# A pad of 256 instead of 192 bytes in front of the second and third stage's tiles

## The chip, the core and the metric

The kernel runs on one core of a Trainium2 chip. The metric is the device time of one execution in microseconds (us); lower is better. The core has five engines with instruction queues of their own: TensorE (PE, matrix multiply; its weight loads are listed as PEld), VectorE (DVE), ScalarE (ACT), GpSimd (POOL) and SyncE (SP), which issues the DMAs here. Matmuls read both operands from SBUF, 128 partitions of on-chip memory, and write PSUM. A tile in SBUF has the same byte address in every partition, and "its address" below means that.

## What is computed

One layer of an encoder on 2048 tokens of width 1024 in float32: three token mixers on one normalised input, merged by gates, projected into the residual stream, and an MLP.

```
h = rmsnorm(x, g_mix);  z = h @ w_in
h_m   = bidirectional chunkwise mLSTM (4 heads)
h_na  = 2-D neighbourhood attention (8 heads, 32 x 64 grid)
h_mem = cross-attention into 256 memory tokens (4 heads)
gates = sigmoid(gate_pre)
y = gates[0] * (h_m @ w_proj_mlstm) + gates[1] * (h_na @ w_proj_na) + gates[2] * (h_mem @ w_proj_mem)
x = x + y @ w_out
u = rmsnorm(x, g_ffn) @ w_up                    # 1024 -> 4096
return x + square(relu(u)) @ w_down             # 4096 -> 1024
```

## The kernel before

Every large product is taken in the type fp32r with each operand split in two, high part and rest, and three matmuls (high x high, high x rest, rest x high). `mm3` issues them on lines 232, 233 and 234. In `matmul(out, lhs, rhs)` the left operand is the stationary one (128x128, loaded as weights), the right one is moving (128x512). The profile's names give the moving operand first: `mm<-X,ws` streams from X against weights of a ws tile. Where both operands are in the same tile one name stands, `mm<-X`. Lines 232 and 233 share a stationary operand, 234 has the rest part.

The work runs in three stages, each with a pool of tiles of its own in the same part of SBUF (`p1`, `p2`, `p3` in `phases`):

- Stage 1 (`phase_1`): normalisation, the projections of `w_in` block by block (512 tokens each), the attention branches. `tok_group` has moving ws and stationary hT, `ch_group` moving hT and stationary ws.
- Stage 2 (`phase_2`): the mLSTM (`ml_stream`, many small matmuls on the stage's own tiles, lines 773 to 905), and between them the gates of two blocks by `ch_group`.
- Stage 3 (`phase_3`): gates left over (`late_gates`), and then for each of two pairs of blocks: `merge` (8 chunks of 128 channels; branches against projection weights, moving X, stationary ws), `out_proj` (32 groups of 24 matmuls over both pairs; moving ws, stationary hT or X; each followed by four transposes on line 1341 that make operands of the MLP), `mlp_up` (16 rounds) and `mlp_down`.

The MLP's two products are done as 2x2 block products with 7 instead of 8 multiplications. `mlp_up` takes its left operands (weights and their sums) from ws tiles and its right operands from X; one product is 4 k-steps of three matmuls. `mlp_down` takes both from X, where its operands are loaded and split on lines 1463 and 1464. In these loops the order of TensorE's instructions is the order of the program (`manual_schedule`).

What the places in SBUF are:

- The pool `ws` comes first: a pad of 128 bytes at byte 1152, then five buffers of 8448 bytes from 1280 on.
- The pool `h`: hT, 32768 bytes at 43520. The outputs of mlp_up and the sums of mlp_down (`acc`) take its place in turn, and so does the merge's result for one block of a pair.
- The pool `w` (raw weights, three buffers of 4224 bytes) at 76288, the pool `c` (identity, constants, small tiles) at 88960.
- At 96768 begin `p1`, `p2` and `p3` in turn. `p2` and `p3` begin with a pad of `PAD` bytes (`self.pad(self.p_a, PAD)` in `phases`), which is a tile of its own, set to zero once on DVE (line 251). In `p3` the next tile is X: seven places of 2 (high, rest) x 4 x 512 numbers, 114688 bytes. With 192 bytes of pad X begins at 96960. Behind it come small tiles and the eight buffers `ev`.

Slices of these tiles that matmuls read begin whole multiples of 512 bytes into the tile in X, ws and hT alike.

The right operands of the MLP in the code:

```
        def product(p, l, r, first):                                  # mlp_up
            lhs, rhs = w[l], self.X[r]
            for k in range(4):
                self.mm3(p, (lhs[0][:, k], lhs[1][:, k]), (rhs[:, 0, k], rhs[:, 1, k]), ...)
...
                        self.mm3(p, (at[:, 0, d, ts], at[:, 1, d, ts]), (at[:, 0, 2 + d], at[:, 1, 2 + d]), ...)   # mlp_down
```

Of the kernel before, what the change touches and what calls it, by code (L numbers as in the profile page):

```python
# [23 lines left out]
TB = 512  # L24
LOW, LATER, LATER_A, SOON = 100, 60, 60, 40
TICKS_2, START_2 = 4, 20
PAD = 192
EV = {1: 2, 2: 2, 3: 8}
XT = 2
PREP_V = 2  # L30
# [50 lines left out]
class Body:  # L81
# [176 lines left out]
    def phases(self):  # L258
# [7 lines left out]
        with tc.tile_pool(name="p2", bufs=1) as self.p_a:  # L266
            self.pad(self.p_a, PAD)
            self.ev_bufs = EV[2]
            self.psum(self.phase_2, mm=2, pn=4, mx=2)
        with tc.tile_pool(name="p3", bufs=1) as self.p_a:  # L270
            self.pad(self.p_a, PAD)
            self.ev_bufs = EV[3]
# [1305 lines left out]
```

## Time and profile before

| | |
|---|---|
| median of 3 runs | 2993.33 us (2991.52 to 2995.25) |
| the profiled execution | 2998.03 us |
| its span, first to last instruction | 2996.3 us |
| mean granted TensorE clock | 0.994 |
| weights, intermediates and results moved by DMA | 632.97 MB, mean 211 GB/s |

The page lists for each engine its busy time, its share of the span and its instructions; then the chain of work that ended last, followed back from the end; then groups of instructions by line: operation, tiles (output and inputs), shape, count, busy time, mean duration, and idle time of the engine before them with what ended it. A matmul's bar is longer than the distance to the next matmul, since they are pipelined: the timeline (start, length, engine, line, operation) shows starts, and the view by windows gives busy time and counts within chosen stretches, the granted clock, and the mean busy share of the 16 DMA engines.

### The profile page before, as it was taken

How to read it: one execution, taken by the hardware profiler on the slowest of the kernel's cores; microseconds unless marked ns; L12 is line 12 of the kernel's file. 1: busy time of each engine (PE TensorE's matmuls, PEld its weight loads, DVE VectorE, ACT ScalarE, POOL GpSimd, SP SyncE). 2: the span in 40 equal slices, each digit the busy share in tenths (PEclk: the TensorE clock that was granted, in tenths of full speed). 3: DMA queues.
4: the chain of work that ended last, by engine and by line, in shares of the span. 5: the costliest groups of instructions: out<-in, count | busy, mean ns of one | idle time of the engine just before them, and what ended most of it. 6: DMA issues, size and time to landing. Idle time of an engine off the chain costs nothing.

```text
span 2996.3 us, 41916 instructions
## 1 busy us (share of the span) xinstructions
PE 2929.4 (98%) x15028; PEld 2375.1 (79%) x15028; DVE 2066.5 (69%) x3523; ACT 1195.8 (40%) x2198; POOL 268.8 (9%) x423
## 2 busy tenths in 40 slices
PE   8999999999989899999999999999999999999999
PEld 6888888778777677778888888888778888888887
DVE  6676864476654766765688878666675987885665
ACT  6465654355543333342243333533312433334331
POOL 4121200021001323420000000000000000000000
PEclk9999999999999999999999999999999999999999
DMA  8786877876998667788444445766863444466554
GB/s 276 222 275 200 242 231 246 275 215 203 289 283 267 199 202 236 247 275 306 141 132 161 144 149 178 256 195 218 280 209 119 148 151 146 142 223 226 191 185 165
DMA packets 341712, 632.97 MB, mean 211 GB/s; under 512 B 29344, under 2 KB 151008, under 8 KB 341504
## 3 DMA queue, kind: packets, MB, share of 16 engines
q1 hardware_dynamic: 341504, 630.30, 65.5%
q8 instruction: 118, 1.93, 0.3%
q14 instruction: 90, 0.74, 0.1%
HBM read 453.63 MB, written 176.55 MB: 210 GB/s over the span
## 4 chain that ended last, share of the span: by engine, by line
PE 55%; DVE 2%; DMA 2%; issue 1%; ACT 0%; POOL 0%; SPq 0%; DVEq 0%; ACTq 0%; POOLq 0%
PE mm L232 18%; PE mm L233 18%; PE mm L234 18%; PE mm L1341 0%; DMA wr<-in_w_units_dram 0%; DMA hf<-s_hf 0%; DVE h L901 0%; DMA og<-s_o 0%; DVE ev L1497 0%; DVE acc L1490 0%; ACT hf L897 0%; POOL rs L325 0%; DMA X<-s_a 0%; DVE ws L177 0%; DVE h L889 0%
## 5 line engine op out<-in xcount | busy, mean ns | idle before, releaser
L232 PE MATMUL mm<-X,ws 128*128 128x512 f32 x1152 | 455.7, 396 | 0.0
L234 PE MATMUL mm<-X,ws 128*128 128x512 f32 x1152 | 455.4, 395 | 0.0
L233 PE MATMUL mm<-X,ws 128*128 128x512 f32 x1152 | 455.4, 395 | 0.0
L232 PE MATMUL mm<-hT,ws 128*128 128x512 f32 x896 | 375.0, 419 | 8.2 <-DMA hT<-s_hT 4.4
L177 DVE TENSOR_TENSOR ws<-wr,ws 128x1024 fp32r<-128x1024 f32 (+1 forms) x212 | 264.5, 1254 | 136.2 <-ACT ws L176 132.6
L234 PE MATMUL mm<-hT,ws 128*128 128x512 f32 x896 | 353.2, 394 | 0.0
L233 PE MATMUL mm<-hT,ws 128*128 128x512 f32 x896 | 353.2, 394 | 0.0
L233 PE MATMUL mm<-X 128*128 128x512 f32 x896 | 349.6, 390 | 3.4 <-DVE X L1464 3.4
L234 PE MATMUL mm<-X 128*128 128x512 f32 x896 | 349.3, 390 | 0.5 <-DVE X L1464 0.5
L232 PE MATMUL mm<-X 128*128 128x512 f32 x896 | 349.3, 390 | 0.0
L1463 ACT ACTIVATE X<-X 128x1024 fp32r<-128x1024 f32 x176 | 186.6, 1062 | 324.7 <-DMA X<-s_t 115.7
L1464 DVE TENSOR_TENSOR X<-X 128x1024 fp32r<-128x1024 f32 x176 | 214.6, 1224 | 136.7 <-ACT X L1463 135.8
L176 ACT ACTIVATE ws<-wr 128x1024 fp32r<-128x1024 f32 (+1 forms) x212 | 223.4, 1058 | 163.8 <-PE mm L234 88.9
L232 PE MATMUL mm<-ws,hT 128*128 128x512 f32 (+2 forms) x704 | 259.8, 369 | 2.7 <-ACT zif L524 1.8
L234 PEld LDWEIGHTS mm<-X,ws 128*128 128x128 f32 x1152 | 216.4, 188 | 52.3
L232 PEld LDWEIGHTS mm<-X,ws 128*128 128x128 f32 x1152 | 216.4, 188 | 52.2
L233 PEld LDWEIGHTS mm<-X,ws 128*128 128x128 f32 x1152 | 216.5, 188 | 52.1
L234 PE MATMUL mm<-ws,hT 128*128 128x512 f32 (+2 forms) x704 | 249.6, 355 | 2.0 <-DVE hT L434 2.0
L233 PE MATMUL mm<-ws,hT 128*128 128x512 f32 (+2 forms) x704 | 248.9, 354 | 0.0
L202 ACT ACTIVATE ws<-wr 128x512 fp32r<-128x512 f32 x224 | 135.1, 629 | 229.8 <-PE mm L234 148.8
L232 PEld LDWEIGHTS mm<-hT,ws 128*128 128x128 f32 x896 | 170.1, 190 | 49.7 <-issue 10.7
L234 PEld LDWEIGHTS mm<-hT,ws 128*128 128x128 f32 x896 | 169.6, 189 | 38.9
(266 smaller groups left out, 4865.8 us busy)
## 6 DMA issues: line engine op xcount, KB each, us to landing
wr<-in_w_units_dram SPq DMA_DIRECT2D x308, 512.0 KB
s_s<-u SPq DMA_DIRECT2D x32, 1024.0 KB
X<-s_s SPq DMA_DIRECT2D x64, 512.0 KB
X<-s_t SPq DMA_DIRECT2D x64, 512.0 KB
s_g<-ev SPq DMA_DIRECT2D x96, 256.0 KB
ev<-s_g SPq DMA_DIRECT2D x96, 256.0 KB
s_a<-u SPq DMA_DIRECT2D x96, 256.0 KB
X<-s_a SPq DMA_DIRECT2D x48, 512.0 KB
```

The source lines that it names most:

```text
L176: nc.scalar.activation(w[:, 0], raw, AF.Copy)
L177: nc.vector.tensor_tensor(w[:, 1], raw, w[:, 0].bitcast(F32), ALU.subtract)
L202: nc.scalar.activation(hi, src, AF.Copy)
L232: mm(out, lhs[0], rhs[0], start=first, stop=False)
L233: mm(out, lhs[0], rhs[1], start=False, stop=False)
L234: mm(out, lhs[1], rhs[0], start=False, stop=last)
L1463: nc.scalar.activation(hi, src, AF.Copy)
L1464: nc.vector.tensor_tensor(lo, src, hi.bitcast(F32), ALU.subtract)
```

## The change

The constant `PAD` is 256 instead of 192. It is the size in bytes of the pads at the start of `p2` and `p3`. All tiles of the second and the third stage lie 64 bytes higher; X begins at 97024. Tiles of the pools `ws`, `h`, `w` and `c` and of stage 1 stay where they are. No instruction is added or removed; the two pads' memsets write 64 instead of 48 columns.

```
@@ -24,7 +24,7 @@
 TB = 512
 LOW, LATER, LATER_A, SOON = 100, 60, 60, 40
 TICKS_2, START_2 = 4, 20
-PAD = 192
+PAD = 256
 EV = {1: 2, 2: 2, 3: 8}
 XT = 2
 PREP_V = 2
```

More of the change, by code (lines that the diff above doesn't have):

```diff
@@ L26 @@
 TICKS_2, START_2 = 4, 20
-PAD = 192
+PAD = 256
 EV = {1: 2, 2: 2, 3: 8}
```

## The prediction

> **What bounds the kernel now.** I read the page from the top: engines, then the chain that ended last.
>
> ```profile
> span 2996.3 us, 41916 instructions
> PE 2929.4 (98%) x15028; PEld 2375.1 (79%) x15028; DVE 2066.5 (69%) x3523; ACT 1195.8 (40%) x2198; POOL 268.8 (9%) x423
> PE 55%; DVE 2%; DMA 2%; issue 1%; ACT 0%; POOL 0%; SPq 0%; DVEq 0%; ACTq 0%; POOLq 0%
> L232 PE MATMUL mm<-X,ws 128*128 128x512 f32 x1152 | 455.7, 396 | 0.0
> L232 PE MATMUL mm<-X 128*128 128x512 f32 x896 | 349.3, 390 | 0.0
> ```
>
> The third line is the chain: it was followed back over some 60% of the span, and 55 of these 60 points are TensorE. So a matmul that gets shorter shortens the kernel, as long as nothing else is late. The groups name the moving operand first, then the stationary one. `mm<-X,ws` (X streams, weights come from a ws tile) is merge and mlp_up: 1152 on each of the lines 232, 233 and 234, 3456 in all. `mm<-X` (both operands in X) is mlp_down, 2688 in all.
>
> Busy time says little here, since a matmul's bar is 0.39 us and the next one starts long before it ends. What counts is the step from start to start. The timeline of TensorE gives it wherever an unbroken stretch begins and ends:
>
> ```profile
> 1377.34 0.39 PE L232 MATMUL mm<-X,ws 128*128 128x512 f32 x1
> 1466.94 0.39 PE L232 MATMUL mm<-ws,hT 128*128 128x512 f32 x1
> 1567.55 0.47 PE L232 MATMUL mm<-X,ws 128*128 128x512 f32 x1
> 1875.62 0.39 PE L232 MATMUL mm<-X 128*128 128x512 f32 x1
> 2187.05 0.40 PE L232 MATMUL mm<-X,ws 128*128 128x512 f32 x1
> 2276.64 0.39 PE L232 MATMUL mm<-ws,yT 128*128 128x512 f32 x1
> 2377.14 0.48 PE L232 MATMUL mm<-X,ws 128*128 128x512 f32 x1
> 2685.22 0.39 PE L232 MATMUL mm<-X 128*128 128x512 f32 x1
> ```
>
> The first merge runs from the first row to the second: 8 chunks x 2 blocks x 8 k x 3 = 384 matmuls in 89.60 us, a step of **233.3 ns**. The second (rows five and six) takes 89.59 us for as many. One mlp_up is 16 x 7 products x 12 = 1344 matmuls. 24 of them come before the last transposes, and the other 1320 run from row three to four and from seven to eight: 308.07 and 308.08 us, 233.4 ns.
>
> Now the stretches with another pairing of operands, from the view by windows. Columns: the window and its length, busy us and count of PE, PEld, DVE, ACT and POOL, the granted clock, the DMA share, GB/s.
>
> ```profile
> 1350.50:1377.10 26.60, 26.60 (x119) 22.00 (x118) 5.00 (x5) 5.64 (x8) 0.00 (x0) 1.00 0.95 355
> 1377.50:1466.50 89.00, 89.00 (x384) 71.30 (x383) 69.79 (x102) 19.40 (x25) 0.00 (x0) 1.00 0.71 230
> 1575.00:1875.00 300.00, 300.00 (x1288) 241.70 (x1287) 244.15 (x370) 97.34 (x157) 0.00 (x0) 1.00 0.46 158
> 1880.00:2080.00 200.00, 200.00 (x884) 165.62 (x883) 124.87 (x133) 83.35 (x88) 0.00 (x0) 1.00 0.68 222
> 2384.00:2684.00 300.00, 300.00 (x1287) 241.75 (x1286) 243.17 (x370) 97.81 (x157) 0.00 (x0) 1.00 0.46 159
> 2690.00:2980.00 290.00, 290.00 (x1281) 240.23 (x1280) 187.97 (x206) 113.45 (x117) 0.00 (x0) 1.00 0.61 198
> ```
>
> A window also counts the bars that reach into it, about 0.39/0.23 = 1.7. On mlp_up the correction gives 300/(1288 - 1.7) = 233.2 ns, as the timeline did. The late gates (first row, moving hT, stationary ws) step by 26.60/117.3 = **226.8 ns**. mlp_down (fourth and sixth rows) steps by 200/882.3 = 226.7 and 290/1279.3 = 226.7. The clock is 1.00 in all six rows and PE is busy throughout. So the same instruction, 128x512 fp32r, has two steady steps, 226.7 and 233.3 ns.
>
> The program's map of SBUF puts ws buffers at byte 1280 of each partition (5 x 256) and every 8448 after it (33 x 256), hT at 43520 (170 x 256), X at 96960 = 378 x 256 + 192. All slices used begin whole multiples of 512 bytes into their tile. So within 256 bytes the pairs (moving, stationary) stand at (0, 0) in the late gates, (192, 192) in mlp_down and (192, 0) in merge and mlp_up. Where the two agree the step is 226.7, where they differ it is 233.3. The sharpest comparison is that of the late gates with the merge right behind them: both take their weights from units in ws, and only the moving tile changes.
>
> **The change, part by part.** X moves to 96768 + 256 = 97024 = 379 x 256. Every pair above becomes (0, 0).
>
> Merge and mlp_up: 3456 matmuls x (233.3 - 226.7 = 6.6 ns) = 22.8 us, of which merge has 768 x 6.6 = 5.1 and mlp_up 2688 x 6.6 = 17.7. Ends of this unknown: nothing at one side (233.3 stays), 226.7 at the other, the fastest steady step of the trace. I take 226.7, because the gates and mlp_down both reach it and (0, 0) is what the gates have.
>
> mlp_down goes from (192, 192) to (0, 0). Both have 226.7, so 0; the end against it is that it falls to 233.3, 2688 x 6.6 = 17.7 us lost, for which no row speaks.
>
> The output projection has moving ws and, for half of its 32 groups, a stationary X: the pair is (0, 192) and becomes (0, 0). Here are a group with stationary hT and one with stationary X, each from its first matmul to the transposes behind it:
>
> ```profile
> 1478.20 0.48 PE L232 MATMUL mm<-ws,hT 128*128 128x512 f32 x1
> 1483.78 0.60 PE L1341 MATMUL mm<-ident,ev 128*128 128x128 f32 x4
> ...
> 1490.07 0.48 PE L232 MATMUL mm<-ws,X 128*128 128x512 f32 x1
> 1495.66 0.60 PE L1341 MATMUL mm<-ident,ev 128*128 128x128 f32 x4
> ```
>
> 5.58 and 5.59 us for 24 matmuls: 16 groups x 0.01 = 0.2 us, at most 16 x (5.59 - 24 x 0.2267) = 2.4. I take 0.2. That even the agreeing pair needs 5.58 where 24 x 0.2267 would be 5.44 shows that a stretch after an interruption starts with longer steps, 0.14 us in all. mlp_up and merge have next to none of these.
>
> The second stage's tiles move by 64 bytes too. Its window and its most frequent small groups:
>
> ```profile
> 925.00:1346.00 421.00, 392.52 (x2149) 298.90 (x2148) 266.87 (x524) 156.96 (x415) 130.09 (x172) 0.98 0.74 233
> L863 PE MATMUL pn<-v,pt 128*128 128x129 f32 x256 | 43.1, 293 | 0.0
> L866 PE MATMUL pn<-C,qw 64*128 64x129 f32 x240 | 29.6, 323 | 0.0
> L872 PE MATMUL mx<-v,kw 128*64 128x129 f32 x240 | 19.9, 285 | 3.3 <-DVE hm L908 3.3
> ```
>
> hT and ws stay where they are. The tiles of this stage stay together, and only their distance to ws, hT and the identity changes. Of the 2149 matmuls 736 are those three groups. If each gained or lost a whole 6.6 ns it would be 4.9 us either way; their distances are of many kinds, and the stage has 28.5 us in which TensorE waits. I take 0 and keep 5 us at each side.
>
> The two pads become 64 instead of 48 floats wide: one memset each.
>
> ```profile
> L251 DVE MEMSET pad<- x3: 85/98/98, 0.9 to 1353.2; 128x48 f32 x2, 128x32 f32 x1
> 1353.22 1.74 SPq L1271 DMA_DIRECT2D X<-s_hm  x4
> 1367.90 1.70 SPq L1271 DMA_DIRECT2D X<-s_hmem  x2
> ```
>
> 85 to 98 ns, 13 more for 16 columns, beside TensorE's work: 0. No DMA, wait or queue position is added. The loads into X are issued from 1353.2 to 1369.6, while the merge that reads them starts at 1377.34 without a wait, so an extra microsecond there is hidden.
>
> What is late next: TensorE does the same work in 3% less time, so DVE rises from 244 to 244 of 291.4 us per window in mlp_up, 81 to 84%, and DMA from 0.46 to 0.47; in merge DVE goes from 78 to 81%, DMA from 0.71 to 0.73. Both stay below TensorE.
>
> Sum: 22.8 + 0.2 = **23.0 us**. The profiled span 2996.3 becomes 2973.3, and the execution that carries it 2998.03 becomes 2975.0. That execution is 4.7 above the median of 2993.33; the steps are hardware steps in both, so 2993.33 - 23.0 gives **2970.3**.
>
> **The rivals.** (1) *Distance, not alignment.* Every fast pair is also one of neighbours (hT beside ws, X with X), and every slow pair takes one operand from each end of SBUF. If that is the reason, the change does nothing: 2993.3. Against it: stationary X with moving ws is just as far apart, and the 5.59 us group is hardly slower than its neighbour. 7%.
>
> (2) *The load of the neighbours.* DVE is busy 19% of the gates' window and 62 and 65% of mlp_down's, but 78 and 81% in merge and mlp_up. If DVE's traffic stretches the steps, nothing changes either: 2993.3. Against it: between 19 and 65% the step does not move at all. 4%. Beside this stands the Trainium skill, "TensorE: Matmul & The Clock Gate", section "Step-by-step: what each phase is for": TensorE has two independent read ports, and loading the next weights takes no read bandwidth from the running matmul. By that rule the places of the two operands cannot matter and the sum would be 0. The two steps at one granted clock do not disprove it, but they need another reason then.
>
> (3) *DVE becomes the bound in mlp_up.* If its queue runs late once in each of the 32 rounds (16 per pair), each costs the 0.14 us of a restart: 4.5 us back, 18.5 gained, 2974.8. If it restarts in each of the 224 products the gain falls by up to 17.7, to merge's 5.1 + 0.2, but 84% busy speaks against that. A middle case, half of the gain (11.5), is 2981.8. 8% for this rival.
>
> (4) *Slower.* Equal places could make the two streams hit the same part of memory when they come from different tiles. The place is merge and mlp_up; at the price of as much again as the excess seen, 6.6 ns, they go to 239.9: 22.8 us lost, 3016. It decides the sign once the step there exceeds 233.3. Against it: hT and ws are different tiles at (0, 0) and step by 226.8. 4%.
>
> **How the numbers follow.** Forecast 77%, (1) 7%, (2) 4%, (3) 8%, (4) 4%. Around the forecast the second stage's 5 and the projection's 2.4 give 2963 to 2976. Adding (3) up to half of the gain, the range ends at 2982. Below 2963 and above 2982 are some 15 to 20%. A measurement of this kernel tells about 0.2%, 6 us, from no change. Faster: 77 + 8 = 85%; same: 11%; slower: 4%.
>
> **What would show it.** In the profile after, the first merge should take 384 x 226.7 = 87.1 us instead of 89.60, the unbroken part of mlp_up 1320 x 226.7 = 299.3 instead of 308.07; mlp_down's windows keep 226.7, and the `mm<-ws,X` groups 5.58. A merge that is fast and an mlp_up with idle time in its L232 rows is rival 3. A step of 233.3 in both is rivals 1 or 2. It would be wrong altogether if mlp_down's step left 226.7 or if stage two's window moved by more than 5 us.

## The result, and the profile after

| | before | after |
|---|---|---|
| median of runs (range) | 2992.89 us (2991.52 to 2995.25, 4 runs) | 2974.45 us (2966.35 to 2976.35, 4 runs) |
| the profiled execution | 2998.03 us | 2974.11 us |
| its span | 2996.3 us | 2972.4 us |

The ratio is 0.9932, with a 95% interval of 0.9913 to 0.9952: 0.5 to 0.9% faster. The forecast was 2970.3 us, in a range of 2963 to 2982.

First the page of the changed kernel: span, engines, the chain that ended last by engine, and the group of merge and mlp_up.

```profile
span 2972.4 us, 41917 instructions
PE 2906.3 (98%) x15028; PEld 2373.9 (80%) x15028; DVE 2061.5 (69%) x3523; ACT 1195.7 (40%) x2198; POOL 264.1 (9%) x423
PE 54%; DVE 2%; DMA 2%; issue 1%; ACT 0%; SPq 0%; POOL 0%; DVEq 0%; ACTq 0%; POOLq 0%
L232 PE MATMUL mm<-X,ws 128*128 128x512 f32 x1152 | 448.5, 389 | 0.0
L232 PE MATMUL mm<-X 128*128 128x512 f32 x896 | 349.5, 390 | 0.0
```

TensorE still bounds the kernel, with the same 15028 matmuls, and is busy for 98% of the span as before. Of the two groups only `mm<-X,ws` has shorter bars, 389 instead of 396 ns; `mm<-X` has not. One instruction more is counted (41917 against 41916): a semaphore instruction of GpSimd in the second stage, of which more below. The timeline of TensorE, the same eight matmuls as in the prediction (start, length, engine, line, operation):

```profile
1374.22 0.39 PE L232 MATMUL mm<-X,ws 128*128 128x512 f32 x1
1461.26 0.39 PE L232 MATMUL mm<-ws,hT 128*128 128x512 f32 x1
1561.81 0.47 PE L232 MATMUL mm<-X,ws 128*128 128x512 f32 x1
1861.13 0.39 PE L232 MATMUL mm<-X 128*128 128x512 f32 x1
2173.94 0.39 PE L232 MATMUL mm<-X,ws 128*128 128x512 f32 x1
2260.98 0.39 PE L232 MATMUL mm<-ws,yT 128*128 128x512 f32 x1
2362.02 0.48 PE L232 MATMUL mm<-X,ws 128*128 128x512 f32 x1
2661.32 0.39 PE L232 MATMUL mm<-X 128*128 128x512 f32 x1
```

Subtracting these starts, and those of before, splits the whole span into stretches with the same instructions on TensorE:

| stretch | before, us | after, us | difference |
|---|---|---|---|
| start to the first merge (stages 1 and 2, late gates) | 1377.34 | 1374.22 | -3.1 |
| first merge, 384 matmuls | 89.60 | 87.04 | -2.6 |
| output projection, start of mlp_up | 100.61 | 100.55 | -0.1 |
| mlp_up, 1320 matmuls | 308.07 | 299.32 | -8.8 |
| mlp_down | 311.43 | 312.81 | +1.4 |
| second merge | 89.59 | 87.04 | -2.6 |
| output projection, start of mlp_up | 100.50 | 101.04 | +0.5 |
| mlp_up | 308.08 | 299.30 | -8.8 |
| mlp_down and the end | 311.08 | 311.08 | 0.0 |

Merge now steps by 87.04/384 = 226.7 ns, mlp_up by 299.3/1320 = 226.7. The four stretches give 22.6 us, the 48 matmuls of mlp_up that lie before the 1320 give 0.3 more by the same step, and the rest of the 23.9 is spread over stretches that go both ways. The +1.4 of the first mlp_down is not the change's: a second profile of the changed kernel (below, "the change again") has 311.00 us there, and in that stretch TensorE waits for DVE to split operands (line 1464), 3.9 us before and 4.4 after.

The view by windows for merge, mlp_up and mlp_down (window and length, busy us and count of PE, PEld, DVE, ACT and POOL, clock, DMA share, GB/s):

```profile
1375.00:1461.00 86.00, 86.00 (x381) 71.22 (x380) 69.36 (x102) 18.94 (x25) 0.00 (x0) 1.00 0.73 236
1570.00:1860.00 290.00, 290.00 (x1282) 240.11 (x1281) 242.58 (x369) 96.35 (x155) 0.00 (x0) 1.00 0.47 163
1880.00:2080.00 200.00, 200.00 (x884) 165.62 (x883) 126.07 (x135) 81.25 (x85) 0.00 (x0) 1.00 0.65 213
```

In merge DVE is at 69.36/86 = 81% and DMA at 0.73, in mlp_up at 242.58/290 = 84% and 0.47. TensorE is busy for the whole of each window, so neither of them has become the bound. mlp_down has the count that it had, 884 in 200 us.

### The profile page after: what moved, and what is told of

The parts are those of the page before. It is cut to its first block, busy times and chain, and to the rows that moved or that the text cites. A ratio compares the mean times of both kernels' runs of the same rounds, so it can differ in the third digit from the quotient of the medians.

```text
span 2972.4 us, 41917 instructions
## 1 busy us (share of the span) xinstructions
PE 2906.3 (98%) x15028; PEld 2373.9 (80%) x15028; DVE 2061.5 (69%) x3523; ACT 1195.7 (40%) x2198; POOL 264.1 (9%) x423
## 4 chain that ended last, share of the span: by engine, by line
PE 54%; DVE 2%; DMA 2%; issue 1%; ACT 0%; SPq 0%; POOL 0%; DVEq 0%; ACTq 0%; POOLq 0%
PE mm L233 18%; PE mm L234 18%; PE mm L232 18%; DMA og<-s_o 1%; DVE h L901 1%; PE mm L1341 0%; DMA hf<-s_hf 0%; DMA wr<-in_w_units_dram 0%; DVE ev L1497 0%; ACT hf L897 0%; DVE acc L1490 0%; POOL rs L325 0%; DVE h L889 0%; DMA X<-s_a 0%; DVE ws L177 0%
## 5 line engine op out<-in xcount | busy, mean ns | idle before, releaser
L232 PE MATMUL mm<-X,ws 128*128 128x512 f32 x1152 | 448.5, 389 | 0.0
L234 PE MATMUL mm<-X,ws 128*128 128x512 f32 x1152 | 448.2, 389 | 0.0
L233 PE MATMUL mm<-X,ws 128*128 128x512 f32 x1152 | 448.1, 389 | 0.0
L177 DVE TENSOR_TENSOR ws<-wr,ws 128x1024 fp32r<-128x1024 f32 (+1 forms) x212 | 262.3, 1244 | 137.7 <-ACT ws L176 136.7
L176 ACT ACTIVATE ws<-wr 128x1024 fp32r<-128x1024 f32 (+1 forms) x212 | 223.3, 1058 | 163.8 <-PE mm L234 90.8
```

What stands on the lines that cost most here:

```text
L176: nc.scalar.activation(w[:, 0], raw, AF.Copy)
L177: nc.vector.tensor_tensor(w[:, 1], raw, w[:, 0].bitcast(F32), ALU.subtract)
L232: mm(out, lhs[0], rhs[0], start=first, stop=False)
L233: mm(out, lhs[0], rhs[1], start=False, stop=False)
L234: mm(out, lhs[1], rhs[0], start=False, stop=last)
```

## Experiments

Each edit is against the changed kernel (PAD = 256), and each kernel computes the whole layer. Theory A is that of the prediction: what counts is where the moving operand lies against the stationary one, within 256 bytes. Theory B takes the change at its word: the moving operand has to begin at a multiple of 256 bytes.

**Everything at 192.** ws, hT and X all begin 64 bytes below a multiple of 256; X is where it was before the change.

```
-            self.pad(self.p_ws, 128)
+            self.pad(self.p_ws, 64)
```

> The pad in front of ws is 64 instead of 128 bytes, PAD stays 256: ws, hT and X all begin at 192 within 256 bytes, so every pair (moving, stationary) of the large matmuls is (192, 192), and X is where it was before the change. Theory A (only the distance between the two operands within 256 bytes counts): first merge 87.04 us and the unbroken part of mlp_up 299.3, as after the change; the late gates stay at 226.8 ns a step; span 2972, within 6. Theory B (the moving operand has to begin at a multiple of 256 bytes): merge 89.6 and mlp_up 308.1 as before the change, the gates go to 233.3 ns, span 2995 or more.

The timeline: a matmul of the late gates, 116 before the first merge, then first merge and first mlp_up:

```profile
1338.18 0.39 PE L233 MATMUL mm<-hT,ws 128*128 128x512 f32 x1
1364.48 0.39 PE L232 MATMUL mm<-X,ws 128*128 128x512 f32 x1
1451.52 0.39 PE L232 MATMUL mm<-ws,hT 128*128 128x512 f32 x1
1552.11 0.47 PE L232 MATMUL mm<-X,ws 128*128 128x512 f32 x1
1851.42 0.39 PE L232 MATMUL mm<-X 128*128 128x512 f32 x1
```

87.04 and 299.31 us, to 0.01 what the change gives, with no large operand at a multiple of 256. The late gates keep their step as well. Windows of this kernel, the gates and mlp_down:

```profile
1337.70:1364.20 26.50, 26.50 (x118) 21.95 (x117) 5.02 (x5) 5.58 (x8) 0.00 (x0) 1.00 0.94 354
1860.00:2060.00 200.00, 200.00 (x884) 165.64 (x884) 124.62 (x133) 84.28 (x89) 0.00 (x0) 1.00 0.66 222
```

The late gates' window gives 26.50/(118 - 1.7) = 227.9 ns, where one matmul more in the count would make it 225.9. The starts are sharper: (1364.48 - 1338.18)/116 = 226.7 ns. mlp_down is at 226.7 too. Theory B is wrong. The span, 2961.0 us, lay 5 below the expected band: this run was faster in its first two stages, of which more below.

**The moving operand at a multiple of 256, the weights not.**

```
-PAD = 256
+PAD = 320
-            self.pad(self.p_ws, 128)
+            self.pad(self.p_ws, 64)
```

> The pad in front of ws is 64 bytes and PAD 320: ws and hT at 192, X at 0, so merge and mlp_up have the pair (0, 192), with the moving operand at a multiple of 256 bytes. Theory A: they are slow, over 87.6 us for the first merge and over 301 for mlp_up, and take the same as the kernel with X at 64 and ws at 0, since both distances are 64. Theory B: 87.04 and 299.3, as after the change. mlp_down stays at 226.7 ns by both.

**The weights at a multiple of 256, X 64 above one.**

```
-PAD = 256
+PAD = 64
```

> PAD 64: X at 64 within 256 bytes, ws at 0. Theory A: the same times for the first merge and mlp_up as the kernel with ws at 192 and X at 0, both above 87.6 and 301 us; if only the size of the distance counted and not its sign, 89.6 and 308.1 like 192. Theory B: slow too, 89.6 and 308.1. mlp_down 226.7 ns a step by theory A (its pair is 64, 64), slow by theory B.

The timeline of the kernel with ws at 192 and X at 0, and then of the one with ws at 0 and X at 64:

```profile
1368.87 0.40 PE L232 MATMUL mm<-X,ws 128*128 128x512 f32 x1
1456.78 0.40 PE L232 MATMUL mm<-ws,hT 128*128 128x512 f32 x1
1557.93 0.48 PE L232 MATMUL mm<-X,ws 128*128 128x512 f32 x1
1860.17 0.39 PE L232 MATMUL mm<-X 128*128 128x512 f32 x1
```

```profile
1366.57 0.40 PE L232 MATMUL mm<-X,ws 128*128 128x512 f32 x1
1454.48 0.40 PE L232 MATMUL mm<-ws,hT 128*128 128x512 f32 x1
1555.63 0.48 PE L232 MATMUL mm<-X,ws 128*128 128x512 f32 x1
1857.87 0.39 PE L232 MATMUL mm<-X 128*128 128x512 f32 x1
1870.00:2060.00 190.00, 190.00 (x840) 157.39 (x839) 117.54 (x125) 79.39 (x85) 0.00 (x0) 1.00 0.66 222
```

Both kernels take 87.91 us for the merge and 302.24 for mlp_up, equal to 0.01. Their operands lie at different places, and only the distance from the weights to X, 64 bytes, is common to them. This is theory A as sharply as it can be put: a moving operand at a multiple of 256 is slow if the weights are 64 below one. The last line is mlp_down with X at 64: 190/(840 - 1.7) = 226.7 ns, since both of its operands moved together. The sign of the distance counts (always from the weights up to the moving operand): with X 64 bytes above the weights a step takes 228.9 ns, with X 192 above (which is 64 below, within 256) 233.3. The output projection, where X is the stationary operand, shows the same from the other side. Its groups of 24 with stationary X take 5.59 us (median of 16) in the kernel before, where the moving operand lies 64 above the weights within 256, but 5.68 and 5.69 in the kernels with X at 64 and with X at 0 and ws at 192, where it lies 192 above; with the change they take 5.58.

**Other distances:** `PAD = 128`, `PAD = 32` and `PAD = 224`, with ws at 0.

> PAD 128: X at 128 within 256 bytes, ws at 0. Theory A with a period of 256 bytes: first merge over 87.6 us and mlp_up over 301. With a period of 128 bytes: 87.04 and 299.3, and the 256 of the change is more than is needed. Theory B: 89.6 and 308.1.

> PAD 32: X at 32 within 256 bytes, ws at 0, the smallest distance that the tiles' places allow. Theory A with a price that grows with the distance: first merge between 87.04 and 87.91 us (0 and 64), mlp_up between 299.3 and 302.2. If any distance but 0 costs alike: 87.91 and 302.2. If places within a line of 64 bytes count as the same: 87.04 and 299.3.

> PAD 224: X at 224 within 256 bytes, ws at 0, which is 32 bytes below the next multiple. If the price depends on the distance in one direction (0, 64, 128, 192: 87.04, 87.91, 89.59, 89.60 us for the first merge), it stays near 89.6 and 308. If it is the distance to the nearest multiple that counts, it equals the kernel with X at 32.

The timeline again, first merge and first mlp_up, of the kernels with 128, 32 and 224:

```profile
1369.43 0.40 PE L232 MATMUL mm<-X,ws 128*128 128x512 f32 x1
1459.03 0.39 PE L232 MATMUL mm<-ws,hT 128*128 128x512 f32 x1
1560.09 0.48 PE L232 MATMUL mm<-X,ws 128*128 128x512 f32 x1
1866.92 0.39 PE L232 MATMUL mm<-X 128*128 128x512 f32 x1
```

```profile
1369.02 0.40 PE L232 MATMUL mm<-X,ws 128*128 128x512 f32 x1
1458.62 0.40 PE L232 MATMUL mm<-ws,hT 128*128 128x512 f32 x1
1559.76 0.48 PE L232 MATMUL mm<-X,ws 128*128 128x512 f32 x1
1867.84 0.40 PE L232 MATMUL mm<-X 128*128 128x512 f32 x1
```

```profile
1364.90 0.40 PE L232 MATMUL mm<-X,ws 128*128 128x512 f32 x1
1454.51 0.39 PE L232 MATMUL mm<-ws,hT 128*128 128x512 f32 x1
1555.63 0.48 PE L232 MATMUL mm<-X,ws 128*128 128x512 f32 x1
1863.71 0.39 PE L232 MATMUL mm<-X 128*128 128x512 f32 x1
```

The merges take 89.60, 89.60 and 89.61 us, mlp_up 306.83, 308.08 and 308.08. Put together (where two kernels have one distance, their stretches agree to 0.03):

| X above the weights, within 256 bytes | first merge, us | step, ns | mlp_up (1320), us |
|---|---|---|---|
| 0 | 87.04 | 226.7 | 299.3 |
| 32 | 89.60 | 233.3 | 308.1 |
| 64 | 87.91 | 228.9 | 302.2 |
| 128 | 89.60 | 233.3 | 306.8 |
| 192 (before) | 89.60 | 233.3 | 308.1 |
| 224 | 89.61 | 233.3 | 308.1 |

At 128 the first merge takes 89.60 us, so the period is not 128 bytes. Nor is it 512: the buffers of ws lie 33 x 256 bytes apart, so that with the change X stands at odd and even multiples of 256 above them by turns, and all steps of the merge are 226 or 227 ns. For 32 bytes all three expectations were wrong: the smallest distance tried costs as much as the largest, more than 64. There is no price that grows with the distance. 224 came out equal to 32, which the second reading foresaw, and at 89.6, which the first foresaw, so it tells the two apart no further.

The whole times of these six kernels, one run each: 2962.75 us with everything at 192, 2975.85 with ws at 192 and X at 0, 2970.66 with X at 64 and 2987.91 at 128, on a chip where the kernel before took 2985.92; 2991.82 at 32 and 2986.63 at 224, where it took 2991.46. They hold stages 1 and 2 as well, which vary by more than some of these differences (below), so the argument rests on the stretches.

**Only the second stage's pad.** The third stage keeps 192, X stays where it was before the change.

```
         with tc.tile_pool(name="p3", bufs=1) as self.p_a:
-            self.pad(self.p_a, PAD)
+            self.pad(self.p_a, 192)
```

> The pad is 256 bytes in front of the second stage's tiles and 192 in front of the third's: the half of the change that does not touch X. Theory A: the first merge 89.60 us, mlp_up 308.1, as before the change; the second stage 357.9 as after it, within 5, since its large matmuls' operands do not move; all of the gain is gone but what the second stage has. If the other order of instructions in the second stage carried the gain: merge and mlp_up slow and the span still 20 us shorter.

```profile
1365.49 0.39 PE L232 MATMUL mm<-X,ws 128*128 128x512 f32 x1
1455.09 0.39 PE L232 MATMUL mm<-ws,hT 128*128 128x512 f32 x1
1555.83 0.48 PE L232 MATMUL mm<-X,ws 128*128 128x512 f32 x1
1863.91 0.40 PE L232 MATMUL mm<-X 128*128 128x512 f32 x1
```

Merge and mlp_up are back at 89.60 and 308.08 us, though the second stage has the change's order of instructions; so it is not that order that shortens the steps. The second stage's mLSTM took 356.0 us from its first to its last matmul, against 357.9 with the change: within the 5 expected. Its one time, 2986.57 us, is 4.9 below the kernel before on the same chip (2991.46), and its first row shows where that is from: the first merge starts at 1365.49 us, 8.7 earlier than in the profile of the change. Up to the third stage both kernels have the same instructions in the same order on every engine and the same places in SBUF. So 8.7 us is what two executions of the same stages 1 and 2 can differ by, perhaps on different chips, and the 3.1 us in the first line of the table of stretches can't be laid to the change.

**Timed together:** the change again (6 runs), only the third stage's pad, everything at 192, and the identity at a multiple of 256 (4 runs each), with the kernel before on the same chip (2989.88 us, 2984.69 to 2993.04, 11 runs). The edits of the second and fourth:

```
         with tc.tile_pool(name="p2", bufs=1) as self.p_a:
-            self.pad(self.p_a, PAD)
+            self.pad(self.p_a, 192)
```

```
-             tc.tile_pool(name="w", bufs=1) as self.p_w, \
              tc.tile_pool(name="c", bufs=1) as self.p_c, \
+             tc.tile_pool(name="w", bufs=1) as self.p_w, \
```

> The changed kernel once more, timed in more rounds: the steps say 22.7 us (2 x 2.56 in merge, 2 x 8.77 in mlp_up), that is a ratio of 0.9924 to the kernel before. If the second stage and the stalls in the first mlp_down move systematically as well, the ratio lies off that by more than 0.001.

> The pad is 192 bytes in front of the second stage's tiles and 256 in front of the third's: the half of the change that moves X. Theory A: merge 87.04 and mlp_up 299.3 us, ratio 0.9924 as for the whole change, within 0.001. If the second stage's part of the change was worth its 2.3 us: 0.9932.

> All large operands at 192 within 256 bytes again, timed in more rounds: ratio 0.9924 as for the change by theory A, within 0.001; 0.990 if the shorter first two stages of its single profile (970.8 and 353.1 us) are its own and not that run's.

> After the change, and the pool c opened ahead of the pool w, so that the identity lies at a multiple of 256 bytes (76288) instead of 128 off it. Merge, mlp_up and mlp_down as after the change. If the long steps that follow the transposes (5.58 us for 24 matmuls of the output projection in place of 5.44) come from the place of the identity, the output projection's 101 us fall by up to 16 x 0.14 = 2.2 and the first two stages by some us; if they come from the interruption itself, nothing changes.

> The change with the identity at a multiple of 256 bytes, timed in more rounds: ratio 0.9924 as for the change if the place of the identity is worth nothing, and lower by 0.0003 for the 0.9 us by which its output projections were shorter than those of the change in one profile each (100.4 and 100.2 us against 100.6 and 101.0).

| kernel | median, us | ratio to before, 95% interval |
|---|---|---|
| the change again | 2968.65 (2964.00 to 2976.44) | 0.9931 (0.9918 to 0.9945) |
| only the third stage's pad | 2964.99 (2962.98 to 2967.28) | 0.9918 (0.9905 to 0.9931) |
| everything at 192 | 2964.43 (2960.97 to 2965.30) | 0.9914 (0.9901 to 0.9927) |
| the change, identity at a multiple of 256 | 2965.12 (2963.19 to 2967.74) | 0.9919 (0.9906 to 0.9932) |

All four intervals hold 0.9924, the ratio that the steps alone give, and they overlap each other, so no kernel can be called better than the change. The profile of the kernel with only the third stage's pad:

```profile
1364.90 0.39 PE L232 MATMUL mm<-X,ws 128*128 128x512 f32 x1
1451.94 0.39 PE L232 MATMUL mm<-ws,hT 128*128 128x512 f32 x1
1552.30 0.48 PE L232 MATMUL mm<-X,ws 128*128 128x512 f32 x1
1851.59 0.39 PE L232 MATMUL mm<-X 128*128 128x512 f32 x1
```

87.04 and 299.29 us. So half of the change, the pad of the third stage, carries all of the gain that can be seen. Whether the second stage's half costs up to 3.7 us (2968.65 - 2964.99) stays open; against it speaks that the last two kernels of the table have the second stage's wider pad and its order of instructions too, at 2964.43 and 2965.12 us. For everything at 192, the 0.990 that was expected if its short first two stages were its own lies just outside the interval, and its second profile reaches the first merge at 1367.98 us instead of 1364.48.

The identity's place is worth nothing that shows. In the single profile the first output projection with the start of mlp_up runs between these rows:

```profile
1458.73 0.39 PE L232 MATMUL mm<-ws,hT 128*128 128x512 f32 x1
1559.10 0.48 PE L232 MATMUL mm<-X,ws 128*128 128x512 f32 x1
```

100.37 us, against 100.55 with the change, and a group of 24 takes 5.58 us in both. The one run took 2968.62 us. The reading by which the projections fall by up to 2.2 is not met, so the place of the identity alone does not make the long steps after transposes; their cause stays open.

## Why the prediction was right

- *The bound and the step.* The chain of TensorE said that a shorter step shortens the kernel by as much, and it did: 22.6 us of steps in a span shorter by 23.9. The step of 226.7 ns, taken from the late gates and mlp_down, came out in merge and mlp_up to the last digit: 87.04 against 87.1 foretold, 299.3 against 299.3.
- *The reason.* Both operands at the same place within 256 bytes gave the short step before the change, at (0, 0) and (192, 192). The kernel with everything at 192 and the pair with a distance of 64 show that it is this distance and no place by itself. That the change names multiples of 256 is one way to get it. One sentence of the prediction was too coarse: "where they differ it is 233.3". A distance of 64 costs 2.2 ns instead of 6.6. The sum did not need that sentence, since its 6.6 was read at the very distance that the change removes; a forecast for a kernel with another distance would have been off by it. The groups `mm<-ws,X`, at a distance of 64 and with 0.01 us to gain, were the row that spoke against it.
- *mlp_down.* Costed at 0: its second run takes 311.08 us up to the end in both kernels, and the window of the first has the same 884 in 200 us.
- *The output projection.* Costed at 0.2 us gained; -0.1 and +0.5 were measured in its two runs. The groups themselves went from 5.592 to 5.584 us (medians of 16), 0.1 in all; the term is smaller than what the whole stretch can show.
- *The second stage.* Costed at 0 within 5: its mLSTM took 357.9 us instead of 360.2 from first to last matmul, and 354.4 in the second profile of the change. That is inside what the same code varies by, so the 0 is neither confirmed nor refuted.
- *Rival 1, distance across SBUF.* X and ws are as far apart as before and the step fell. *Rival 2, the load of DVE.* DVE's share rose to 81 and 84% and the step fell. Both are out. *Rival 3.* No idle time of TensorE in the windows of mlp_up. *Rival 4.* Different tiles at (0, 0) do not collide.
- *The rule of the Trainium skill* ("TensorE: Matmul & The Clock Gate", "Step-by-step: what each phase is for") that loading weights takes no read bandwidth from the running matmul: by the prediction's reading of it the sum would have been 0, and it was not. Here the step depends on where the weights lie against the moving operand, by up to 6.6 ns of 226.7, at a granted clock of 1.00. So the two are not independent for the fp32r operands of this kernel, whatever they share; that it is read bandwidth was not shown.
- *What was not seen.* "No DMA, wait or queue position is added" was not right as to positions. The wider memset of the second stage's pad takes 112 instead of 98 ns, and in the program after it a few rows on DVE, ACT and SP stand in another order at the start of that stage (L750, L754 and L177 on DVE; L176 and L763 on ACT; L172, L797 and L806 among SP's), and GpSimd has one semaphore instruction more (L849). So "no instruction is added", as the change was described, does not hold to the last one. The kernel with the third stage's pad alone keeps the order of before. No price of it could be measured.
- *The remaining 4.2 us* between 2970.3 and the median of 2974.45 are no term of the sum. Four runs of the changed kernel span 2966 to 2976. In the second series the gain is 2989.88 - 2968.65 = 21.2 us, in the first 18.4; both intervals hold the 23.0 forecast (a ratio of 0.9923).

## What to carry to other kernels

Where a matmul kernel is bound by TensorE, measure the step from start to start in stretches without interruption, by pairs of tiles; two steady values for the same instruction ask for a look at the addresses. Put the tiles that serve as moving and stationary operands of the same matmuls at the same place within 256 bytes (fp32r, 128x512: 226.7 ns a step, against 228.9 to 233.3 otherwise); one pad does it. To judge a change of under 1% compare stretches between the same matmuls, since the stages around them took up to 12 us more or less on the same instructions, half of this effect.

## What the runs showed that was not expected

- The price of the distance is neither monotonic nor graded: 32, 192 and 224 bytes cost 6.6 ns a step, 64 cost 2.2. At 128 the stretches do not even agree with each other: 89.60 us in the first merge (233.3 ns), 89.23 in the second, 306.83 in mlp_up (232.4). By the starts in the traces the steps there repeat in short cycles: 229 and 238 ns by turns in the merge at 128, 231 and 236 in mlp_up before the change, and 226, 229 and 232 at 64. The 226 of that last cycle falls on line 233 in mlp_up of the kernel with X at 64 and on line 234 in that with ws at 192 and X at 0, with the same total, so it is not one of the three matmuls that is slow. Why the cycles arise was not tested, nor whether weight load and moving operand meet in some part of the memory, nor distances below 32 bytes, nor which of the neighbouring matmuls' weights count.
- The same stages 1 and 2, on one and the same sequence of instructions and places, took 8.7 us more or less (the change and the kernel with the second stage's pad alone) and even 12.4: the first merge starts at 1377.34 us in the kernel before and at 1364.90 in that with the third stage's pad alone, which are alike up to there.
